# Whole feature tiles instead of half tiles in layer 1's modulation products on TensorE

## The chip, the cores and the metric

One core of a Trainium2 chip runs the whole program as one launch. The time is device microseconds of that core, the median of three runs; lower is better. The engines are named as the profile names them: PE (TensorE's matmuls), PEld (its weight loads), DVE (VectorE), ACT (ScalarE), POOL (GpSimd) and SP (SyncE).

## The reference, cut to what matters

A two layer network with 1024 features works on 512 latent and 256 context tokens. Layer 0 mixes tokens with a gated linear recurrence, layer 1 with latent attention; each is followed by a gated MLP. Everything is modulated: six vectors of 1024 features a layer, each for two conditions (c and c_ctx), come from

```python
silu_c = jax.nn.silu(c)
mod_lat = jnp.split((silu_c @ ada_w[i] + ada_b[i])[:, None, :], 6, axis=-1)
mod_ctx = jnp.split(silu_cc @ ada_w[i] + ada_b[i], 6, axis=-1)
h_lat = _modulate(_rmsnorm(x, norm_mix_g[i]), mod_lat[0], mod_lat[1])
x = x + mod_lat[2] * o_lat
```

`ada_w` is 2 x 1024 x 6144 in float32. Channels 0 and 1 (shift and scale of the first norm) are needed for both conditions in layer 1; its channels 2 to 5 are needed for the latent tokens alone.

## The kernel before, in words

Every matrix product is done in float32 by three passes over a high and a low part (`hh`/`hl`, `wh`/`wl`, `ah`/`al`). Activations are held with the features on the 128 partitions and the 768 tokens along the free axis. Weights come in on SP's queue as `raw` tiles, ACT copies their high part (L108), DVE or POOL subtracts to the low part (L119). The order of the program is written out by hand; each engine works its own instructions off in that order.

The modulation vectors are made in small steps that `ada_step` (L583) puts between other products. `adas` (L225, L227) lists the weight tiles in the order of their use: whole tiles of 128 x 1024 for layer 0's channels 2 to 5, half tiles of 128 x 512 for layer 1, in the order channel, half, k (the eight blocks of 128 input features). `ada_fill` (L232) issues their loads on POOL's queue (L239 for half tiles, L242 for whole ones), up to `used + bufs` tiles ahead; a new load takes the buffer of the tile read longest ago, so it waits for that tile's readers. In layer 0's MLP there are three buffers for half tiles.

`ada_product` (L563) is the step on PE: `csil[:, k, :]` (128 x 32) is the stationary operand, and four matmuls for the four feature quarters of a tile write to four groups of 32 partitions of `psada`, accumulated over k. `ada_sum` (L533) is the step on DVE for one condition alone, one multiply and add over 512 columns (L538 for k = 0, L540 else), whose sum `ada_add` (L544) brings across partitions with the matmuls of L554. Layer 1's channels 0 and 1 go through PE, its channels 2 to 5 through DVE. After a channel's last k `ada_copy` (L558) copies `psada` to SBUF on ACT (L560); `ada_evac` (L508) transposes it on PE (L519) at the third `ada_step` after that and adds the bias on DVE (L525). `ada_until` (L596) does at once what is missing up to a channel.

Layer 0's MLP is `ffn0` (L1136). Four hidden tiles are made plainly (`plain`, L1263), the others two by two blocks by a Strassen scheme of seven products (`pair`, L1224; its matmuls L1166). Six groups of 4, 2, 4, 4, 4, 4 hidden tiles follow each other; behind each group the eight output tiles m = 0 to 7 add their part of the result (L1212, residuals L767). Six PSUM banks hold output tiles, two for each. Layer 1's steps stand in these places: one after each of the plain tiles 1, 2 and 3 (L1288 to L1297), two in each pair while channels 0 and 1 last (`on_pe`, L1222; L1234 and L1246), one otherwise, and behind every output tile (L1333):

```python
on_pe = lambda: ada_state["used"] < 8 * KT
ada_step(1 if nh < 4 or on_pe() else 2)
```

In front of the last group's output tiles stands `ada_until(1, 4)` (L1307).

Of the kernel before, what the change touches and what calls it, by code (L numbers as in the profile page):

```python
# [12 lines left out]
ALU = mybir.AluOpType  # L13
# [4 lines left out]
KT = D // P  # L18
# [127 lines left out]
def kernel(ctx, tc, x, c, ctx_in, c_ctx, ada_w, ada_b, norm_mix_g, norm_ffn_g, ffn_w_in,  # L146
# [4 lines left out]
    act, dve, pe = nc.scalar, nc.vector, nc.tensor  # L151
# [34 lines left out]
    def ps_aux(name):  # L186
        return psx.tile([P, 512], F32, name=name, tag="aux")
# [36 lines left out]

    adas = [(0, ch, k) for ch in range(2, 6) for k in range(KT)]  # L225

    adas += [(1, ch, k, half) for ch in range(6) for half in range(2) for k in range(KT)]  # L227
    N_ADA = [4 * KT, 14 * KT, 16 * KT]
    ada_tiles = {}
    ada_state = {"loaded": 0, "used": 0, "evac": None, "sums": None, "bufs": NB_ADA}  # L230

    def ada_fill(eng=nc.gpsimd):  # L232
        while ada_state["loaded"] < min(N_ADA[0], ada_state["used"] + ada_state["bufs"]):
            i = ada_state["loaded"]
            l, ch, k, *half = adas[i]
            if half:
                c0 = ch * D + half[0] * 512
                t = ada_state["pool"].tile([P, 512], F32, name=f"ada{i}", tag="ada", bufs=3)
                eng.dma_start(t, ada_w[l, k * P:(k + 1) * P, c0:c0 + 512])  # L239
            else:  # L240
                t = ada_pool.tile([P, 1024], F32, name=f"ada{i}", tag="ada")
                eng.dma_start(t, ada_w[l, k * P:(k + 1) * P, ch * D:(ch + 1) * D])  # L242
            ada_tiles[i] = t
            ada_state["loaded"] += 1
# [209 lines left out]
    csil = const.tile([P, KT, 32], F32, name="csil")  # L454
# [15 lines left out]
    mod = const.tile([P, 2, 6, 2, KT], F32, name="mod")  # L470
    gm = const.tile([P, 4, 2, KT], F32, name="gm")
    adab = lambda l, ch: cols_b[:, l * 48 + ch * 8:l * 48 + ch * 8 + 8]
# [5 lines left out]
    ada_ps = {}  # L478
# [29 lines left out]
    def ada_evac(wait=False):  # L508

        if ada_state["evac"] is None:  # L510
            return
        i, l, ch, sb = ada_state["evac"]
        if wait and ada_state["calls"] < 2:
            ada_state["calls"] += 1
            return
        ada_state["evac"] = None
        px = ps_aux(f"adax{i}")
        for cc in range(2):
            pe.transpose(px[:, cc * P:(cc + 1) * P], sb[:, cc * P:(cc + 1) * P], ident)  # L519

        order = "p (c j) -> p c j" if l and ch < 2 else "p (j c) -> p c j"
        n = dict(c=2, j=4)
        pv = px[:, :256].rearrange("p (c j r) -> p c j r", r=32, **n)
        for v in range(2):
            dve.tensor_tensor(mod[:, l, ch, v, :].rearrange(order, **n), pv[:, :, :, v],  # L525
                              adab(l, ch).rearrange(order, **n), op=ALU.add)
        if ch in (1, 4):
            w = l + (2 if ch == 4 else 0)
            for v in range(2):
                dve.scalar_tensor_tensor(gm[:, w, v, :], mod[:, l, ch, v, :], 1.0, gcol(w),  # L530
                                         op0=ALU.add, op1=ALU.mult)

    def ada_sum(i, t, l, ch, k, half):  # L533


        total, col = acc[:, :512], csil[:, k, 0:1]
        if k == 0:
            dve.tensor_scalar(total, t, col, None, op0=ALU.mult)  # L538
        else:
            dve.scalar_tensor_tensor(total, t, col, total, op0=ALU.mult, op1=ALU.add)  # L540
        if k == KT - 1:
            ada_state["sums"], ada_state["calls"] = (i, l, ch, half, total), 0

    def ada_add():  # L544
        if ada_state["sums"] is None:
            return
        i, l, ch, half, total = ada_state["sums"]
        ada_state["sums"] = None
        if half == 0:
            ada_ps["half"] = psa.tile([P, 512], F32, name=f"psada{i}", tag="ada")  # L550
        ps = ada_ps["half"]
        for j in range(2):
            r = 64 * half + 32 * j
            pe.matmul(ps[r:r + 32, :256], pick[:, 0, :], total[:, j * 256:(j + 1) * 256], start=True, stop=True)  # L554
        if half == 1:
            ada_copy(i, l, ch, ps)

    def ada_copy(i, l, ch, ps):  # L558
        sb = ada_state["sb"](i)
        act.activation(sb, ps[:, :256], AF.Copy)  # L560
        ada_state["evac"], ada_state["calls"] = (i, l, ch, sb), 0

    def ada_product(i, t, l, ch, k, half=None):  # L563

        n = 256 if half is None else 128
        if k == 0 and not half:
            ada_ps[0] = psa.tile([P, 512], F32, name=f"psada{i}", tag="ada")
        o = (half or 0) * n
        for j in range(4):
            pe.matmul(ada_ps[0][32 * j:32 * j + 32, o:o + n], csil[:, k, :], t[:, j * n:(j + 1) * n],  # L570
                      start=k == 0, stop=k == KT - 1)
        if k == KT - 1 and half != 0:
            ada_copy(i, l, ch, ada_ps[0])

    def ada_one():
        ada_fill()
        i = ada_state["used"]
        l, ch, *f = adas[i]
        (ada_sum if l and ch > 1 else ada_product)(i, ada_tiles.pop(i), l, ch, *f)
        ada_state["used"] += 1  # L580
        ada_fill()

    def ada_step(n=1):  # L583

        if ada_state["sums"]:
            ada_state["calls"] += 1
            if ada_state["calls"] < 2:
                return
            ada_add()
        else:  # L590
            ada_evac(True)
        for _ in range(n):
            if ada_state["used"] < N_ADA[0] and not ada_state["sums"]:
                ada_one()

    def ada_until(l, ch):  # L596
        n = sum(1 for a in adas if a[:2] <= (l, ch)) - ada_state["used"]
        for _ in range(n):
            ada_add()
            ada_evac()  # L600
            ada_one()
        if n >= 0:
            ada_add()
            ada_evac()
# [361 lines left out]
    gel, used = {}, []  # L966
# [169 lines left out]
    def ffn0(na, nb, nxt):  # L1136
        ga, gb = na.group, nb.group
        with ExitStack() as es:
# [64 lines left out]
            def out_tile(c, m, groups, ks, ps=None):  # L1203
                h0, nh, outs = s0_out[c]
                per = 8 // nh
                wh, wl = st.get(outs[m // per])
                ps = ps or {g[0]: ps_bank(f"fo0{c}{m}{g[0]}")[:, :g[1].stop - g[1].start] for g in groups}
                for k in ks:
                    o = k * (1024 // nh) + m % per * P
                    for q, (w, x) in enumerate(((wh, ah), (wh, al), (wl, ah))):  # L1210
                        for v, s in groups:
                            pe.matmul(ps[v], w[:, o:o + P], x[:, k, s], start=k == 0 and q == 0,  # L1212
                                      stop=k == nh - 1 and q == 2)
                return ps
# [7 lines left out]
            on_pe = lambda: ada_state["used"] < 8 * KT  # L1222
# [79 lines left out]
            for c, (h0, nh, outs) in enumerate(s0_out):  # L1302
                for j in range(max(h0, PLAIN0), h0 + nh):
                    pair(j, j - h0, j == h0 + nh - 1)
                lastp = c == len(s0_out) - 1
                if lastp:
                    ada_until(1, 4)  # L1307
                    for m in range(KT):
                        ps = out_tile(c, m, (ga,), range(nh))
                        residual(m, lambda s: ps[1], 0, 5, ga, True)  # L1310
                        if m == 0:
                            st.flush()
                    st.low_engine = nc.gpsimd

                    def last(m):
                        ps = out_tile(c, m, (gb,), range(nh))
                        residual(m, lambda s: ps[0], 0, 5, gb, True)
                        out_done(c, m)

                    boundary([lambda m=m: last(m) for m in range(KT)], nxt, at=(1, 2, 1))  # L1320
                    return

                n0 = nh - 1 if c else 2
                three = [out_tile(c, m, (gb, ga), range(n0)) for m in range(3)]
                for m in range(KT):
                    if m < 3:
                        ps = out_tile(c, m, (gb, ga), range(n0, nh), three[m])
                    else:
                        ps = out_tile(c, m, (gb, ga), range(nh))
                    for g in (gb, ga):  # L1330
                        residual(m, lambda s: ps[g[0]], 0, 5, g, False)
                    out_done(c, m)
                    ada_step(1 if nh < 4 or on_pe() else 2)  # L1333

    na1 = Norm(1, 1, 0, CTXG, hh, hl, "m1a")
    nb1 = Norm(1, 1, 0, LATG, hh, hl, "m1b")
# [419 lines left out]
```

## Time and profile before

| what | value |
|---|---|
| runs of before, us | 1565.91, 1568.83, 1569.62; median 1568.83 |
| the profiled execution, us | 1571.79 |
| its span from the first to the last instruction, us | 1569.9 |
| PE busy, us | 1512.2 |
| DVE, ACT, POOL busy, us | 934.2, 675.9, 281.5 |
| mean granted clock of TensorE | 0.985 |

The profile is of one execution, a little above the median of the runs. A busy PE isn't PE at its peak, since the ends of matmuls are modelled; a product's price is therefore read from the starts of the instructions around it. A matmul in float32 leaves two records. In a line of the timeline the first number is the start, the second how long the merged instructions last, and the bracket tells how long the engine was idle before and what ended that.

### The profile page before, as it was taken

Reading aid. Unit: us, or ns where it says so; the run is one execution under the profiler, and the core shown is the slowest. Engines: PE = TensorE matmul, PEld = TensorE weight load, DVE = VectorE, ACT = ScalarE, POOL = GpSimd, SP = SyncE. Lnnn points to the kernel's source line nnn. Section 1 sums busy time; section 2 is a strip of 40 time slices with the busy share of each in tenths; the row PEclk is TensorE's granted clock in tenths of the full one; section 3 lists DMA queues with packets and bytes.
Section 4 is the critical chain, followed back from the end, with each engine's and each line's share of the span. In section 5 each row is a group of like instructions: output and inputs, shape, how many; then the busy total and the mean of one; then the engine's idle time right before and its main releaser. Section 6 shows DMA issues by size and latency. Waiting matters only on the chain.

```text
span 1569.9 us, 21629 instructions
## 1 busy us (share of the span) xinstructions
PE 1512.2 (96%) x8903; PEld 1321.4 (84%) x8903; DVE 934.2 (60%) x1397; ACT 675.9 (43%) x989; POOL 281.5 (18%) x261
## 2 busy tenths in 40 slices
PE   7999998979999999999999998999998999999998
PEld 5877876868878898999989887899998888888887
DVE  5766778686855657767587457666537543233234
ACT  5486555734423241433424343766644322232223
POOL 3223333242010101001010332111144100000002
PEclk9999999989999999999999999999999999999999
DMA  9434333131233334333242112110112433223222
GB/s 359 127 108 135 108 122 120 59 103 48 68 108 114 104 112 128 114 114 122 94 141 64 51 56 69 29 43 28 54 54 75 161 118 104 81 98 117 81 69 93
DMA packets 134995, 155.14 MB, mean 99 GB/s; under 512 B 6252, under 2 KB 112353, under 8 KB 134897
## 3 DMA queue, kind: packets, MB, share of 16 engines
q1 hardware_dynamic: 122272, 112.21, 22.3%
q0 software_dynamic: 12320, 41.02, 8.2%
q8 instruction: 70, 1.15, 0.3%
q10 hardware_dynamic: 304, 0.53, 0.1%
q14 instruction: 29, 0.23, 0.0%
HBM read 151.64 MB, written 2.10 MB: 98 GB/s over the span
## 4 chain that ended last, share of the span: by engine, by line
PE 82%; DVE 11%; ACT 4%; issue 1%; DMA 1%; SPq 0%; POOL 0%; DVEq 0%; ACTq 0%; POOLq 0%
PE f L791 14%; PE fo L1212 11%; PE x L1166 10%; PE fo L791 8%; PE z L1166 5%; PE lo L791 3%; PE s L1555 3%; PE ga L791 2%; PE wo L791 2%; PE y L1166 2%; PE o L1597 2%; PE p L791 2%; PE g L791 2%; DVE yc L899 1%; PE t L1573 1%
## 5 line engine op out<-in xcount | busy, mean ns | idle before, releaser
L108 ACT ACTIVATE wh<-raw 128x1024 fp32r<-128x1024 f32 (+3 forms) x247 | 208.5, 871 | 203.9 <-PE fo L1212 64.5
L119 POOL TENSOR_TENSOR wl<-raw,wh 128x1024 fp32r<-128x1024 f32 (+3 forms) x66 | 157.5, 2397 | 328.8 <-ACT wh L108 328.6
L119 DVE TENSOR_TENSOR wl<-raw,wh 128x1024 fp32r<-128x1024 f32 (+2 forms) x181 | 169.3, 948 | 11.8 <-ACT wh L108 11.8
L767 DVE SCALAR_TENSOR_TENSOR xT<-fo,mod,xT 128x512 f32<-128x512 f32 (+1 forms) x124 | 74.1, 626 | 129.8 <-PE fo L1212 66.2
L239 POOL DMA_DIRECT2D ada<-in_ada_w_dram x96 | 51.7, 539 | 465.3 <-PE psada L570 217.9
L791 PE MATMUL f<-hh,wh 128*128 128x512 f32 x320 | 124.7, 390 | 0.0
L791 PE MATMUL f<-hh,wl 128*128 128x512 f32 x320 | 124.5, 389 | 0.0
L791 PE MATMUL f<-hl,wh 128*128 128x512 f32 x320 | 124.5, 389 | 0.0
L785 POOL TENSOR_TENSOR acc<-acc,sq 128x256 f32<-128x256 f32 (+1 forms) x52 | 50.7, 975 | 374.1 <-ACT sq L783 371.9
L1212 PE MATMUL fo<-ah,wh 128*128 128x512 f32 (+1 forms) x352 | 98.3, 345 | 0.9 <-DVE g L1273 0.8
L1212 PE MATMUL fo<-al,wh 128*128 128x512 f32 (+1 forms) x352 | 95.8, 338 | 0.4 <-DVE al L1201 0.4
L1212 PE MATMUL fo<-ah,wl 128*128 128x512 f32 (+1 forms) x352 | 95.3, 337 | 0.0
L1109 DVE TENSOR_TENSOR sg<-sg,f 128x512 f32<-128x512 f32 x20 | 13.7, 687 | 116.4 <-ACT sg L1108 116.4
L1108 ACT ACTIVATE sg<-f 128x512 f32<-128x512 f32 x20 | 12.0, 599 | 148.3 <-PE f L791 148.3
L791 PE MATMUL fo<-ah,wh 128*128 128x512 f32 (+1 forms) x200 | 73.0, 365 | 0.0
L791 PE MATMUL fo<-ah,wl 128*128 128x512 f32 (+1 forms) x200 | 72.7, 364 | 0.0
L791 PE MATMUL fo<-al,wh 128*128 128x512 f32 (+1 forms) x200 | 72.7, 364 | 0.0
L791 PEld LDWEIGHTS f<-hh,wh 128*128 128x128 f32 x320 | 60.1, 188 | 13.2 <-issue 0.8
L791 PEld LDWEIGHTS f<-hh,wl 128*128 128x128 f32 x320 | 60.1, 188 | 12.6
L791 PEld LDWEIGHTS f<-hl,wh 128*128 128x128 f32 x320 | 60.1, 188 | 12.4
L1212 PEld LDWEIGHTS fo<-ah,wh 128*128 128x128 f32 x352 | 56.2, 188 | 12.8 <-issue 4.6
L1212 PEld LDWEIGHTS fo<-al,wh 128*128 128x128 f32 x352 | 56.2, 188 | 8.0 <-DVE al L1201 0.7
(490 smaller groups left out, 4023.3 us busy)
## 6 DMA issues: line engine op xcount, KB each, us to landing
raw<-in_ffn_w_in_dram SPq DMA_DIRECT2D x26, 1024.0 KB, 4.9
ada<-in_ada_w_dram POOLq DMA_DIRECT2D x96, 256.0 KB, 3.1
raw<-in_ffn_w_out_dram SPq DMA_DIRECT2D x19, 1024.0 KB, 4.9
raw<-in_ffn_w_in_dram SPq DMA_DIRECT2D x36, 512.0 KB, 4.7
ada<-in_ada_w_dram POOLq DMA_DIRECT2D x30, 512.0 KB, 4.4
ada<-in_ada_w_dram SPq DMA_DIRECT2D x32, 256.0 KB, 5.5
raw<-in_lru_w_in_dram SPq DMA_DIRECT2D x10, 512.0 KB, 5.3
raw<-in_lru_gate_w_dram SPq DMA_DIRECT2D x16, 256.0 KB, 3.2
```

The costliest lines, as they stand in the source:

```text
L108: nc.scalar.activation(dst(hi), src(self.raw[load]), AF.Copy)
L119: self.low_engine.tensor_tensor(dst(lo), src(self.raw[load]), dst(hi).bitcast(F32), op=ALU.subtract)
L239: eng.dma_start(t, ada_w[l, k * P:(k + 1) * P, c0:c0 + 512])
L767: dve.scalar_tensor_tensor(xT[:, m, s], ps(s) if callable(ps) else ps[:, s], mod[:, l, ch, v, m:m + 1], xT[:, m, s], op0=ALU.mult, op1=ALU ...
L785: accs.append(lambda: nc.gpsimd.tensor_tensor(acc[:, s], acc[:, s], sq, op=ALU.add))
L791: pe.matmul(ps[:, off + s.start:off + s.stop], a, b[:, s], start=first and i == 0, stop=last and i == 2)
L899: dve.scalar_tensor_tensor(y[:, s0:s1], ps[:, s0 + o:s1 + o], convw(tap, k), y[:, s0:s1], op0=ALU.mult, op1=ALU.add)
L1166: pe.matmul(ps, w[:, o:o + P], x[:, k0 + k, s], start=first and k == 0 and q == 0, stop=last and k == 3 and q == 2, skip_group_check=not f ...
L1212: pe.matmul(ps[v], w[:, o:o + P], x[:, k, s], start=k == 0 and q == 0, stop=k == nh - 1 and q == 2)
L1555: pe.matmul(ps[:, o:o + 384], x, y[:, k0:k1], start=j == 0, stop=j == 4)
L1573: pe.transpose(ps[:, j * P:(j + 1) * P], prs[h, b][:, j // 3, j % 3 * P:(j % 3 + 1) * P], ident)
L1597: pe.matmul(ps[:, :256], x[:, t % 4, hs], y[:, t, :], start=t == 0 and j == 0, stop=t == NT - 1 and j == 2)
```

## The change

For layer 1's channels 0 and 1 the order of `adas` becomes channel, k, half. `ada_product` takes a list of tiles: one whole tile for layer 0, two half tiles for layer 1, and does four matmuls of 256 columns with either. A step of layer 1's products so uses two half tiles, which are still loaded one by one. The special order of features in `ada_evac` goes. Behind output tiles, while channels 0 and 1 last, the call stands at every second m (groups of four hidden tiles) or every third (others).

```diff
-    adas += [(1, ch, k, half) for ch in range(6) for half in range(2) for k in range(KT)]
+    adas += [(1, ch, k, half) for ch in range(2) for k in range(KT) for half in range(2)]
+    adas += [(1, ch, k, half) for ch in range(2, 6) for half in range(2) for k in range(KT)]
...
-    def ada_product(i, t, l, ch, k, half=None):
-
-        n = 256 if half is None else 128
-        if k == 0 and not half:
+    def ada_product(i, ts, l, ch, k):
+
+        if k == 0:
             ada_ps[0] = psa.tile([P, 512], F32, name=f"psada{i}", tag="ada")
-        o = (half or 0) * n
+        n = 4 // len(ts)
         for j in range(4):
-            pe.matmul(ada_ps[0][32 * j:32 * j + 32, o:o + n], csil[:, k, :], t[:, j * n:(j + 1) * n],
+            pe.matmul(ada_ps[0][32 * j:32 * j + 32, :256], csil[:, k, :], ts[j // n][:, j % n * 256:j % n * 256 + 256],
                       start=k == 0, stop=k == KT - 1)
-        if k == KT - 1 and half != 0:
+        if k == KT - 1:
             ada_copy(i, l, ch, ada_ps[0])
 
     def ada_one():
         ada_fill()
         i = ada_state["used"]
-        l, ch, *f = adas[i]
-        (ada_sum if l and ch > 1 else ada_product)(i, ada_tiles.pop(i), l, ch, *f)
-        ada_state["used"] += 1
+        l, ch, k, *half = adas[i]
+        n = 1
+        if l and ch > 1:
+            ada_sum(i, ada_tiles.pop(i), l, ch, k, *half)
+        else:
+            n = 1 + l
+            ada_product(i, [ada_tiles.pop(i + j) for j in range(n)], l, ch, k)
+        ada_state["used"] += n
         ada_fill()
...
     def ada_until(l, ch):
         n = sum(1 for a in adas if a[:2] <= (l, ch)) - ada_state["used"]
-        for _ in range(n):
+        end = ada_state["used"] + n
+        while ada_state["used"] < end:
...
-                    ada_step(1 if nh < 4 or on_pe() else 2)
+                    ada_step(1 if nh < 4 else 2) if not on_pe() or m % (2 if nh == 4 else 3) == 0 else None
```

In `ada_evac` every channel now uses the order `"p (j c) -> p j c"` for `mod` and the bias.

## Rows read from the trace of the kernel before

**Rows 1.** The page: span, and busy time of the engines.
```profile
span 1569.9 us, 21629 instructions
...
PE 1512.2 (96%) x8903; PEld 1321.4 (84%) x8903; DVE 934.2 (60%) x1397; ACT 675.9 (43%) x989; POOL 281.5 (18%) x261
```

**Rows 2.** Stretches: length, PE, PEld, DVE, ACT, POOL busy (count), granted clock, DMA share, GB/s.
```profile
433.20:475.00 41.80, 41.04 (x279) 32.82 (x278) 23.26 (x35) 8.68 (x12) 4.84 (x9) 1.00 0.36 104
...
509.60:528.90 19.30, 19.30 (x151) 14.49 (x150) 12.68 (x25) 2.80 (x5) 4.30 (x8) 1.00 0.35 101
```

**Rows 3.** One tile's instructions (`psada`), and PE's timeline around one half tile.
```profile
L570 PE MATMUL psada<-ada,csil x512: 272/338/403, 60.4 to 600.4; 128*32 128x256 f32 x86, 128*32 128x128 f32 x85
...
442.28 0.51 PE L1212 MATMUL fo<-al,wh 128*128 128x512 f32 x2
442.63 0.51 PE L1212 MATMUL fo<-ah,wl 128*128 128x512 f32 x2
443.07 0.43 PE L570 MATMUL psada<-ada,csil 128*32 128x128 f32 x8
443.43 0.61 PE L1212 MATMUL fo<-ah,wh 128*128 128x512 f32 x2
```

**Rows 4.** PE's timeline around one whole tile of layer 0, and around two.
```profile
59.92 0.51 PE L791 MATMUL p<-hh,wl 128*128 128x512 f32 x2
60.36 0.64 PE L570 MATMUL psada<-ada,csil 128*32 128x256 f32 x8
60.93 0.50 PE L791 MATMUL g<-hh,wh 128*128 128x512 f32 x1
...
87.50 0.51 PE L791 MATMUL g<-hh,wl 128*128 128x512 f32 x2
87.94 1.07 PE L570 MATMUL psada<-ada,csil 128*32 128x256 f32 x16
88.94 0.50 PE L791 MATMUL ga<-uh,wh 128*128 128x512 f32 x1
```

**Rows 5.** PE's timeline at the start of group 0's output tiles.
```profile
434.40 0.50 PE L1212 MATMUL fo<-ah,wh 128*128 128x512 f32 x1 [0.76 <-DVE g L1273]
```

**Rows 6.** POOL's and SP's timelines; landing: loads from 440 to 480, that at 449.1.
```profile
443.83 0.54 POOL L239 DMA_DIRECT2D ada<-in_ada_w_dram  x1 [9.32 <-PE psada L570]
...
DMA to landing us min/median/max: 2.9/2.9/5.6
...
DMA to landing us min/median/max: 5.6/5.6/5.6
...
448.04 0.99 SPq L350 DMA_DIRECT2D raw<-in_ffn_w_in_dram  x2
```

**Rows 7.** PE's timeline: one sum brought across partitions (two feature quarters).
```profile
619.84 0.62 PE L554 MATMUL psada<-acc,pick 128*32 128x256 f32 x4
```

**Rows 8.** Stretches (columns as in Rows 2): two idle times of PE, and what followed.
```profile
127.20:130.10 2.90, 0.04 (x1) 0.04 (x1) 1.86 (x5) 0.91 (x2) 0.00 (x0) 1.00 0.09 31
130.10:134.20 4.10, 3.73 (x11) 2.93 (x12) 2.64 (x3) 2.67 (x3) 0.00 (x0) 0.59 0.00 0
...
870.70:872.90 2.20, 0.04 (x2) 0.00 (x0) 1.29 (x3) 2.06 (x3) 0.00 (x0) 1.00 0.21 62
872.90:880.00 7.10, 7.08 (x59) 7.08 (x60) 4.21 (x10) 1.53 (x4) 1.47 (x2) 1.00 0.27 74
```

**Rows 9.** PE's and DVE's timelines in front of the last group's output tiles.
```profile
869.84 0.34 PE L1166 MATMUL x<-hh,wl 128*128 128x384 f32 x1
...
872.92 0.44 PE L519 MATMUL adax<-ident,acc 128*128 128x128 f32 x2 [2.18 <-ACT acc L560]
873.12 0.36 PE L1212 MATMUL fo<-ah,wh 128*128 128x256 f32 x1
...
871.68 0.96 DVE L1201 TENSOR_TENSOR al<-g,ah 128x768 fp32r<-128x768 f32 x1 [0.91 <-ACT ah L1200]
```

**Rows 10.** One line's instructions: the sums on DVE.
```profile
L540 DVE SCALAR_TENSOR_TENSOR acc<-ada,csil,acc x56: 741/750/754, 607.2 to 1263.3; 128x512 f32<-128x512 f32 x56
```

More of the change, by code (lines that the diff above doesn't have):

```diff
@@ L519, in ada_evac @@
             pe.transpose(px[:, cc * P:(cc + 1) * P], sb[:, cc * P:(cc + 1) * P], ident)
-        order = "p (c j) -> p c j" if l and ch < 2 else "p (j c) -> p c j"
-        n = dict(c=2, j=4)
-        pv = px[:, :256].rearrange("p (c j r) -> p c j r", r=32, **n)
+        pv = px[:, :256].rearrange("p (c j r) -> p j c r", c=2, j=4)
         for v in range(2):
-            dve.tensor_tensor(mod[:, l, ch, v, :].rearrange(order, **n), pv[:, :, :, v],
-                              adab(l, ch).rearrange(order, **n), op=ALU.add)
+            dve.tensor_tensor(mod[:, l, ch, v, :].rearrange("p (j c) -> p j c", j=4), pv[:, :, :, v],
+                              adab(l, ch).rearrange("p (j c) -> p j c", j=4), op=ALU.add)
         if ch in (1, 4):
```

## The prediction

> **What bounds the kernel now.** I read the page's busy times first. PE is busy for 1512.2 of 1569.9 us [rows 1], so whatever is put into PE's queue, work or wait, moves the end unless PE would have waited there anyway. Then I read the stretches in which layer 1's products run. From the first output tiles of group 0 (433.2 us) to the first Strassen pair, PE is busy for 41.04 of 41.80 us at the full clock; while group 1's output tiles are made (509.6 to 528.9) it is never idle, and DVE is busy for 12.68 of 19.30 us [rows 2]. So in this stage DVE, ACT and POOL have time left and PE has none. The reader is to see in these two groups that a stop of PE here has no later idle time to be made up in.
>
> **The change part by part.** The profiled execution took 1571.79 us (its span is 1569.9), 2.96 us above the median of 1568.83. I sum changes on 1571.8 and take the same sum off the median.
>
> *The products.* The 512 matmul records are two for each matmul: 256 for layer 0's 32 whole tiles and 256 for layer 1's 32 half tiles [rows 3]. A half tile costs what it adds between two output matmul pairs: 443.43 - 442.63, less the 0.35 that separates such pairs (442.63 - 442.28), is 0.45 us [rows 3]. Layer 0 shows the price of what replaces it. A whole tile adds 60.93 - 59.92 - 0.35 = 0.66 us and two in a row 88.94 - 87.50 - 0.35 = 1.09 us [rows 4]: 0.43 for each tile, and some 0.23 for entering and leaving. One of the 32 half tiles costs nothing now, since behind it PE waits 0.76 us for DVE at 434.40 [rows 5]; the whole tile that comes there is 0.21 longer and stays inside that wait. So 31 x 0.45 = 13.95 us go.
>
> What comes is read from the edited call. Three steps after the plain pairs (one of them hidden), two in each of pairs 4 and 5, and m = 0 of group 1 take one tile: 7 x 0.66 = 4.62. In group 0 four heads are processed, so the call there is `ada_step(2)` at m = 0, 2, 4 and 6: the edit dropped `or on_pe()`, which kept this at one. Four doubled steps are 4 x 1.09 = 4.36. Together 3 + 8 + 4 + 1 = 16 tiles. Without any wait PE gains 13.95 - 8.98 = **4.97 us**.
>
> *The wait in the doubled step.* The pool still has three half tile buffers, and `ada_fill` loads up to `used + 3`. A doubled step eats four half tiles. The first product takes two of the three that are there; only then are the buffers refilled; the second product takes the third and one that has just been asked for. POOL can't ask before PE has read the buffer: each such load waits for `psada` [rows 6]. For a half tile the load is issued 0.76 us after the first matmul (443.83 - 443.07, [rows 3, 6]); a whole tile's burst is 0.64 long instead of 0.43 [rows 3, 4], so 0.97. From issue to landing the nine loads of this stretch took 2.9 (lowest), 2.9 (median) and 5.6 us (highest) [rows 6]; the long one was issued at 449.1, a microsecond behind two weight loads on SP at 448.04 [rows 6]. Those weight loads hang on the output tile m = 1, and the doubled step of m = 2 still follows it, so I give m = 2 the long landing and the other three the short one. Behind the landing PE still has two of four feature quarters to do. Two last as long as four side by side: the record of a two-quarter sum is 0.62 long [rows 7], that of a whole tile 0.64, and PE goes on 60.93 - 60.36 = 0.57 us after its start [rows 4]. The wait is then landing + 0.97 + 0.57, less the 1.00 that two tiles take unstopped (88.94 - 87.94): 2.9 gives 3.4, 5.6 gives 6.1. Four of them are 3 x 3.4 + 6.1 = **16.3 us**. Queued behind the waiting matmul is everything on PE, and the residuals on DVE wait for PE; nothing that runs meanwhile shortens PE's own work. Ends of this term: all four short (13.6), all four long (24.4).
>
> The Trainium skill (DMA: Bandwidth & Descriptors, Anatomy of one DMA) fits a GpSimd load as 2.0 us plus its bytes at 436 GB/s, which for 256 KB is an estimate of 2.6 us; by that the four waits would be 4 x 3.1 = 12.4 us. No load of rows 6 was that quick, so the rows decide.
>
> *The clock.* A stop of this length has a price behind it. PE was idle from 127.2 to 130.1 (busy 0.04 of 2.90) and the 4.1 us after that ran at a granted 0.59 of full speed, in part at 1.2 GHz: 0.41 x 4.1 = 1.7 us lost. A shorter idle time, 870.7 to 872.9, was followed by 1.00 [rows 8]. The idle part of our wait is about landing + 0.97 - 1.07 (the doubled burst lasts 1.07), so 2.8 to 5.5 us: nearer to 2.9 than to 2.2. I take 1.7 for each, **6.8 us**, and keep 0 as the other end. [...]
>
> *The sums come earlier.* Tile 64, the first for DVE, is reached at group 1's m = 1 and not in group 2's output tiles. Counting steps on, layer 1's channel 4 is then finished and copied in group 4's output tiles, and `ada_until(1, 4)` in front of the last group finds nothing. There PE now waits 2.18 us for ACT [rows 9]. Without that wait the first output tile starts at 870.0 rather than 873.12, but the last of its four hidden tiles needs `al`, which DVE ends at 871.68 + 0.96 = 872.64 [rows 9]. Twelve matmuls of 0.12 ended at 874.55; now they end near 872.9. Of the 1.65 gained, 0.57 and 0.23 for the sum's matmuls, and some 0.1 for the two transposes, are paid elsewhere, where PE is full: **0.8 us** net.
>
> *At nothing.* DVE does seven sums more in group 1's output tiles, at most 7 x 0.75 = 5.25 us [rows 10], beside 12.68, in 19.3 - 8 x 0.45 + 0.66 = 16.4 us: 1.5 too many. Their cover is the six PSUM banks (three output tiles ahead) and the lighter pairs after them; if that is gone it costs up to 1.5. The loads on POOL's queue are as many and as large as before and POOL does nothing else here. SP's weight loads follow PE as before. The reordering in `ada_evac` changes addresses only.
>
> Sum: 16.3 + 6.8 - 4.97 - 0.8 = +17.3. 1571.8 becomes 1589.1, and the median 1586.1.
>
> **The rivals.** *The half tile is back in time (faster).* If the second product's last half tile has landed when PE gets there, nothing waits: -5.8, 1563.0. It decides at the doubled steps, and breaks even where the four stops with their clock come to 5.8 us, 1.4 each, so landings of about 0.9 us. For it speaks that POOL and half of the DMA capacity are free (share 0.36, [rows 2]); against it the 2.9 us [rows 6].
>
> *The clock stays up.* Stops as above, no loss behind them: 1586.1 - 6.8 = 1579.3. For it: our shortest idle time lies between the 2.2 us that cost nothing and the 2.9 that did [rows 8].
>
> *Every stop is a long one.* Two loads are asked for at once now, and weight loads move with PE: four waits of 6.1 and the clock give 24.4 + 6.8 - 5.8 = +25.4, 1594.2, and with DVE's 1.5 1595.7. For it speaks the one row in nine at 5.6.
>
> *The step isn't doubled*, because the call takes one tile a place after all: then products spill into group 2, no wait arises, and PE's gain of 31 x 0.45 - 15 x 0.66 = 4.1 gives 1564.7. The condition in the diff speaks against it.
>
> **How the numbers follow.** The forecast gets 0.63, the clock that stays up 0.17, long stops 0.12, the landing in time 0.05, the step that isn't doubled 0.03. A measurement of this kernel can tell about 0.3% (4.7 us) from no change. The first three cases lie over that (lowest +7.8: four short stops, no clock loss, all gains), the last two at -4.1 and -5.8, one of them inside the bound. Some hundredths stand for half of my waits being wrong: slower 0.91, same 0.04, faster 0.05. The range goes from 1576, four short stops without clock loss, to 1596, the long stops with DVE's price.
>
> **What would show it.** The profile after should have 128 records of L570 fewer; 16 products; four waits of PE for a DMA into `ada`, in group 0's output tiles, of 3 to 6 us each, every one in its second tile; a lower granted clock behind them; the first sum on DVE right behind group 1's m = 0; and no wait for ACT in front of the last group's output tiles. I am wrong if PE shows no wait for `ada` there, or if these are under 1.5 us each. If they are as I say and the clock stays at 1.00, the second rival holds.

## The result, and the profile after

The changed kernel takes 1587.01 us (median of 4 runs, 1583.17 to 1590.87), the kernel before 1569.22 (4 runs); the ratio is 1.0117, with a 95% interval of 1.0088 to 1.0147. It is slower by 17.8 us, where +17.3 was forecast. Its profiled execution took 1587.94 us, with a span of 1586.1.

The page of the changed kernel, busy times. The program's lines in `ffn0` stand three further on than before (L1212 is now L1215), and L570 is now L567, L554 is L552, L560 is L558, L540 is L538, L239 is L240 and L350 is L351.

```profile
PE 1516.7 (96%) x8775; PEld 1326.7 (84%) x8775; DVE 931.2 (59%) x1397; ACT 676.4 (43%) x989; POOL 281.9 (18%) x261
```

There are 128 PE records fewer than in [rows 1], as forecast. Busy time alone would say that nothing is wrong: 96% as before. What the change did shows in the stretches of its own stage. These are group 0's output tiles, group 1's and group 2's, each from its first output matmul to the first matmul of the next pair; columns are length, then PE, PEld, DVE, ACT and POOL busy (count), granted clock, DMA share and GB/s.

```profile
432.95:495.68 62.73, 48.92 (x256) 37.00 (x257) 19.63 (x29) 6.86 (x11) 9.36 (x18) 0.84 0.35 109
528.22:547.04 18.82, 18.33 (x108) 15.03 (x108) 16.77 (x33) 4.16 (x8) 3.76 (x7) 1.00 0.43 127
606.06:642.25 36.19, 34.48 (x200) 29.65 (x199) 25.28 (x40) 6.11 (x10) 6.06 (x12) 1.00 0.43 129
```

Before, the first of these stretches was

```profile
434.40:472.71 38.31, 38.31 (x257) 30.62 (x257) 20.00 (x30) 6.93 (x11) 3.87 (x8) 1.00 0.38 111
```

So group 0's output tiles take 24.4 us more: PE is idle for 13.8 of 62.73 us, and the granted clock fell from 1.00 to 0.84. All other stages of layer 0's MLP together give 6.9 us back (its whole stretch, from group 0's first output tile to the next layer, went from 474.41 to 491.92 us). The waits of PE between 430 and 640 us in the changed kernel (waited for: us in total, times, longest) name the cause.

```profile
PE psada L567 <- DMA ada<-in_ada_w_dram: 13.3, 4, 5.3
PE psada L552 <- DVE acc L538: 1.7, 1, 1.7
PE fo L1215 <- DVE g L1276: 0.5, 1, 0.5
PE psada L567 <- ACT acc L558: 0.5, 1, 0.5
PE fo L1215 <- DVE al L1204: 0.4, 1, 0.4
```

PE's timeline at the first two doubled steps, m = 0 and m = 2, answers to [rows 3, 4]:

```profile
441.63 1.06 PE L567 MATMUL psada<-ada,csil 128*32 128x256 f32 x12
445.59 0.62 PE L567 MATMUL psada<-ada,csil 128*32 128x256 f32 x4 [2.90 <-DMA ada<-in_ada_w_dram]
446.14 0.94 PE L1215 MATMUL fo<-ah,wh 128*128 128x512 f32 x2
...
452.11 1.06 PE L567 MATMUL psada<-ada,csil 128*32 128x256 f32 x12
458.50 1.07 PE L567 MATMUL psada<-ada,csil 128*32 128x256 f32 x4 [5.34 <-DMA ada<-in_ada_w_dram]
459.50 0.80 PE L1215 MATMUL fo<-ah,wh 128*128 128x512 f32 x1
```

Twelve of sixteen records run at once, the last four wait: one of the four half tiles is not there. The wait for ACT in the table above is at m = 4: there the first product ends channel 0 and the second begins channel 1, and PE waits 0.53 us until ACT has copied `psada`. The half tile came later than that copy, so the copy cost nothing here. POOL's and SP's timelines, with the landing of the loads issued at 442.56 and 453.04, say why; they answer to [rows 6].

```profile
442.56 1.06 POOL L240 DMA_DIRECT2D ada<-in_ada_w_dram  x2 [8.79 <-PE psada L567]
...
DMA to landing us min/median/max: 3.0/3.0/3.0
...
452.31 0.99 SPq L351 DMA_DIRECT2D raw<-in_ffn_w_in_dram  x2
...
453.04 1.59 POOL L240 DMA_DIRECT2D ada<-in_ada_w_dram  x3 [5.99 <-PE psada L567]
...
DMA to landing us min/median/max: 5.4/5.4/5.4
```

The load is issued 0.93 us after the first matmul of the place and lands 3.0 or 5.4 us later; the long one has two weight loads on SP just ahead of it. Behind each stop the clock is down (stretches that begin where the four stops end, columns as above):

```profile
445.60:452.00 6.40, 6.40 (x28) 5.09 (x28) 2.02 (x3) 0.63 (x1) 0.54 (x1) 0.73 0.30 84
458.50:463.30 4.80, 4.80 (x16) 3.40 (x17) 0.00 (x0) 0.00 (x0) 0.54 (x1) 0.50 0.27 87
473.70:477.00 3.30, 3.30 (x11) 2.21 (x12) 0.00 (x0) 0.00 (x0) 0.54 (x1) 0.51 0.40 113
488.20:494.00 5.80, 5.79 (x19) 4.30 (x20) 0.00 (x0) 0.00 (x0) 0.54 (x1) 0.50 0.29 89
```

### The profile page after: what moved, and what is told of

It reads as the page before. It is cut to its first block, busy times and chain, and to the rows that moved or that the text cites. A ratio compares the mean times of both kernels' runs of the same rounds, so it can differ in the third digit from the quotient of the medians.

```text
span 1586.1 us, 21365 instructions
## 1 busy us (share of the span) xinstructions
PE 1516.7 (96%) x8775; PEld 1326.7 (84%) x8775; DVE 931.2 (59%) x1397; ACT 676.4 (43%) x989; POOL 281.9 (18%) x261
## 4 chain that ended last, share of the span: by engine, by line
PE 68%; issue 13%; DVE 12%; ACT 4%; DMA 2%; POOL 1%; SPq 0%; DVEq 0%; POOLq 0%; ACTq 0%
PE f L794 14%; PE fo L794 8%; PE x L1169 7%; PE fo L1215 6%; PE z L1169 4%; PE lo L794 3%; PE s L1558 3%; PE ga L794 2%; PE wo L794 2%; PE o L1600 2%; PE y L1169 2%; PE p L794 2%; PE g L794 2%; DVE yc L902 1%; DMA ada<-in_ada_w_dram 1%
## 5 line engine op out<-in xcount | busy, mean ns | idle before, releaser
L108 ACT ACTIVATE wh<-raw 128x1024 fp32r<-128x1024 f32 (+3 forms) x247 | 208.5, 871 | 208.4 <-PE fo L1215 96.8
L240 POOL DMA_DIRECT2D ada<-in_ada_w_dram x96 | 51.6, 539 | 455.3 <-DVE acc L538 206.4
L1215 PE MATMUL fo<-ah,wh 128*128 128x512 f32 (+1 forms) x352 | 99.6, 349 | 1.1 <-DVE g L1276 0.5
L1215 PE MATMUL fo<-al,wh 128*128 128x512 f32 (+1 forms) x352 | 97.8, 345 | 1.0 <-DVE al L1204 1.0
L1215 PE MATMUL fo<-ah,wl 128*128 128x512 f32 (+1 forms) x352 | 97.3, 343 | 0.0
L1112 DVE TENSOR_TENSOR sg<-sg,f 128x512 f32<-128x512 f32 x20 | 13.8, 688 | 116.7 <-ACT sg L1111 116.7
L1215 PEld LDWEIGHTS fo<-ah,wh 128*128 128x128 f32 x352 | 58.4, 195 | 13.7 <-issue 4.5
L1215 PEld LDWEIGHTS fo<-al,wh 128*128 128x128 f32 x352 | 58.0, 195 | 9.0 <-DVE al L1204 1.5
```

The costliest lines, as they stand in the source:

```text
L108: nc.scalar.activation(dst(hi), src(self.raw[load]), AF.Copy)
L1112: dve.tensor_tensor(sg[:, :n], sg[:, :n], pu[:, off:off + n], op=ALU.mult)
```

## The experiments

The theory is the forecast's: a doubled step eats four half tiles, three are in store, and the fourth is asked for only when PE has read the first, so PE stops for the load and runs at half clock behind it. The rivals are that whole tiles or doubled steps are slow by themselves, that the clock is no part of the price, and that DVE's earlier sums are the bound.

**One tile a place.** Group 0's step isn't doubled; the rest of the program's text is the changed kernel's. The four products left over move to later places, so DVE's first sum starts at 548.23 us instead of 536.45 (606.67 before the change).

```diff
-ada_step(1 if nh < 4 else 2) if not on_pe() or m % (2 if nh == 4 else 3) == 0 else None
+ada_step(1 if nh < 4 or on_pe() else 2) if not on_pe() or m % (2 if nh == 4 else 3) == 0 else None
```

> The doubled steps in group 0 become single ones (every second m still); two products move to pair 6. Theory (a doubled step needs a half tile that was only just asked for): PE waits nowhere for a load into ada, the clock stays at 1.00 through group 0, and the time is that of before less 31 x 0.45 - 15 x 0.66 = 4.1 us and 0.8 us at the last group, some 1564.5 us. Rival (whole tiles as such, their order of loads or the earlier sums on DVE make it slow): still above 1575 us, without long waits.

Measured: 1563.55 us (7 runs), ratio to the kernel before 0.9964 (0.9950 to 0.9979). All waits of PE from 430 to 640 us:

```profile
PE fo L1215 <- DVE g L1276: 0.5, 1, 0.5
PE fo L1215 <- DVE al L1204: 0.4, 1, 0.4
PE psada L552 <- DVE acc L538: 0.3, 1, 0.3
```

No wait for `ada`, and group 0's output tiles take 37.00 us at a clock of 1.00:

```profile
434.56:471.56 37.00, 37.00 (x224) 30.10 (x225) 19.63 (x29) 6.48 (x10) 5.06 (x10) 1.00 0.41 129
```

The rival falls: whole tiles, their order and sums that are earlier than before, if less early than in the changed kernel, are a gain of 0.36%; with the doubled step it is a loss. The next run keeps the early sums.

**Four half tiles in store.** The doubled steps stay.

```diff
+                if ch < 2 and i % 4 == 3:
+                    t = acc[:, :512]
+                else:
+                    t = ada_state["pool"].tile([P, 512], F32, name=f"ada{i}", tag="ada", bufs=3)
...
+        if ada_state["bufs"] > 2:
+            ada_state["bufs"] = 4 if ada_state["used"] < 8 * KT else 3
```

> Doubled steps stay, but there are four half tiles in store while the products last (the fourth lies in the first 512 columns of acc, which are free then). Theory: all four half tiles of a doubled step have landed before it, the four waits of 2 to 5 us and the low clock behind them go, 1564 to 1566 us (DVE may still hold PE up by 1.7 us in group 2). Rival (doubling a step stops PE by something else: the copy of psada on ACT, the residuals on DVE): waits remain in group 0 and the time stays above 1575 us.

Measured: 1565.00 us (8 runs), ratio 0.9972 (0.9962 to 0.9982). Waits of PE from 430 to 640 us (the lines stand five further on than in the changed kernel):

```profile
PE psada L557 <- DVE acc L543: 2.1, 1, 2.1
PE fo L1220 <- DVE g L1281: 0.5, 1, 0.5
PE psada L572 <- ACT acc L563: 0.5, 1, 0.5
PE psada L572 <- DMA ada<-in_ada_w_dram: 0.4, 1, 0.4
PE fo L1220 <- DVE al L1209: 0.4, 1, 0.4
```

With one more half tile in store, 13.3 us of waiting for `ada` become 0.4, and group 0's output tiles take 40.50 us (432.55 to 473.05) instead of 62.73. The stops of 3 to 6 us are not the doubled step's own; they come of too little in store. Some 2 us stay in group 0: read from the starts, the place at m = 2 takes 1.26 us longer than the unstopped 1.00, as a load is still late there, and the one at m = 4 takes 0.74 us longer, where the copy of `psada` on ACT no longer hides behind a load. The longest wait left has nothing to do with group 0: DVE's, in group 2.

**Half tiles, doubled.** The kernel before with the changed kernel's places in group 0.

```diff
-ada_step(1 if nh < 4 or on_pe() else 2)
+ada_step(1 if nh < 4 else 2) if not on_pe() or nh < 4 or m % 2 == 0 else None
```

> The kernel before, with half tiles and their order untouched, but with the places of group 0 as in the changed kernel: every second m, two steps each. Two half tiles are eaten at a place, and three are in store. Theory: no wait for a load, four pairs of half tiles save some 0.2 us each in entering and leaving, so the time of before or 1 us less. Rival (a doubled step in a place stops PE whatever it eats): waits of some us at m = 0, 2, 4, 6 and over 1575 us.

Measured: 1568.68 us (10 runs), ratio 0.9996 (0.9984 to 1.0008): no difference. Here no wait of PE from 430 to 640 us is for `ada`, as a place eats two of three. The same doubling costs nothing with half tiles, where group 0's output tiles take 37.10 us (431.32 to 468.42) against 38.31 before. With whole tiles and three in store it costs 22 us against four in store (62.73 and 40.50).

**Filler in the stops.** Ten matmuls whose result nobody reads, between the two products of a doubled step.

```diff
+    def filler():
+        px = ps_aux("filler")
+        for _ in range(10):
+            pe.matmul(px, hh[:, 0, 0:P], hh[:, 1, 0:512], start=True, stop=True)
...
+                if q and adas[ada_state["used"]][:2] in ((1, 0), (1, 1)):
+                    filler()
                 ada_one()
```

> The changed kernel with ten matmuls of 128x512 whose result nobody reads (some 2.35 us) between the two products of a doubled step. Theory with the clock: they lie inside the waits, which get shorter by as much (0.5 to 1 us left, 3 at m = 2), and PE's clock doesn't fall behind them; of the 8.6 us that the half clock cost, most goes: 1578 to 1581 us. Rival (the clock is no price of the stops): as long as the changed kernel, 1587 us, or longer by the added matmuls.

Measured: 1579.97 us (4 runs), ratio to before 1.0064 (1.0049 to 1.0079). PE still waits 3.9 us for `ada`, 2.4 of them at m = 2:

```profile
PE psada L567 <- DMA ada<-in_ada_w_dram: 3.9, 4, 2.4
```

and group 0's output tiles, at a granted 0.97, take

```profile
433.80:491.07 57.27, 53.33 (x297) 39.65 (x297) 19.60 (x29) 6.83 (x11) 9.32 (x18) 0.97 0.38 120
```

PE does 40 matmuls more and the stretch, whose first output matmul starts at 433.76, is 5.4 us shorter than the changed kernel's 62.73. The loads come no sooner for it: from the first matmul of a place to its last four records PE takes 18.8 us in the four places together, against 18.2 in the changed kernel. So what went is the half clock: it is a price of its own, and the rival falls. One stretch of low clock is left, behind the longest stop.

**A step behind every m.** One whole tile at each output tile of group 0.

```diff
-ada_step(1 if nh < 4 else 2) if not on_pe() or m % (2 if nh == 4 else 3) == 0 else None
+ada_step(1 if nh < 4 or on_pe() else 2)
```

> One whole tile behind every output tile of group 0, as before the call stood. Theory: a place needs one half tile that was asked for at the place before; it is there 0.97 + 2.9 = 3.9 us after that place began, and the place after m = 0 comes 0.66 + 2.22 = 2.9 us later. So one wait of about 1 us at m = 1, up to 2.5 at m = 2 if weight loads come in between, none at m = 3 to 7 (4.4 us apart), no lower clock, some 1565 to 1568 us. Rival (a load is late whenever two half tiles are used at a place): waits at every m.

Measured: 1564.91 us (one run). PE at m = 0 and m = 1:

```profile
442.38 0.64 PE L567 MATMUL psada<-ada,csil 128*32 128x256 f32 x8
442.95 0.61 PE L1215 MATMUL fo<-ah,wh 128*128 128x512 f32 x2
...
446.64 0.63 PE L567 MATMUL psada<-ada,csil 128*32 128x256 f32 x4 [0.79 <-DMA ada<-in_ada_w_dram]
```

The second place waits 0.79 us, where 1 was worked out. At m = 2, where weight loads could have made a wait, none is listed. One of 0.3 us came at m = 3, where none was expected (1.1 us in two waits in all); read from the starts, that place took 1.21 us instead of 0.57, and its load, issued at 450.45, needed 4.8 us to land. In this one run, as in the changed kernel, PE waits by what is missing between the spacing of two places and the way of a load; which load will be a long one was not foreseen.

**Doubled steps at odd m.** m = 1, 3, 5, 7 in place of 0, 2, 4, 6.

```diff
-ada_step(1 if nh < 4 else 2) if not on_pe() or m % (2 if nh == 4 else 3) == 0 else None
+ada_step(1 if nh < 4 else 2) if not on_pe() or (m % 2 == 1 if nh == 4 else m % 3 == 0) else None
```

> The changed kernel with group 0's doubled steps at m = 1, 3, 5, 7 instead of 0, 2, 4, 6. Theory (the 5.3 us wait at m = 2 is long because two weight loads, set off by the output tile m = 1, are issued 0.3 to 0.7 us before its load): the load at m = 1 is now issued before those weight loads, so all four waits are 2 to 3.5 us and at most one stretch of low clock is over 3.4 us. Rival (which landing is long is chance, or the second place is always the long one): one wait of 5 us or more remains.

Measured: 1580.43 us (one run). Waits of PE from 430 to 640 us, and SP's weight loads:

```profile
PE psada L567 <- DMA ada<-in_ada_w_dram: 9.5, 3, 3.2
PE psada L567 <- ACT acc L558: 2.8, 1, 2.8
...
445.65 0.99 SPq L351 DMA_DIRECT2D raw<-in_ffn_w_in_dram  x2
```

No single wait is over 3.2 us, and the longest place, from its first matmul to the next output matmul, takes 5.28 us, where the changed kernel's at m = 2 takes 7.39. The load that the first one waits for was issued at 444.26, ahead of the weight loads, and landed in 3.3 us; the one issued at 445.56 beside them took 5.8, but nobody waited for it. In all eight traces without filler a load issued within 1.1 us of these two weight loads took 4.8 to 5.8 us to land, and the first one in group 0, well ahead of them, 2.8 to 3.7. So the long stop at m = 2 was the weight loads' doing. One stop here is put down to ACT: the channel's copy of `psada` stood behind a weight part (L108) that itself waited 2.1 us for DVE, and the half tile landed 0.8 us after it, so it would have stopped PE anyway.

This run holds a surprise for the clock. Its stretches behind the first, second and fourth stop (3.20, 3.09 and 3.17 us idle):

```profile
447.60:452.00 4.40, 4.40 (x25) 3.48 (x26) 1.79 (x4) 0.00 (x0) 0.54 (x1) 1.00 1.01 316
...
458.80:463.00 4.20, 4.16 (x15) 3.27 (x16) 0.00 (x0) 0.00 (x0) 0.54 (x1) 0.59 0.37 113
...
488.50:493.00 4.50, 4.50 (x30) 3.43 (x31) 0.75 (x2) 0.49 (x1) 1.28 (x3) 1.00 0.75 275
```

Two of these three cost no clock at all, while 2.90 us in the changed kernel did. The third stop, 2.81 us for ACT and 0.8 for the load behind it, was followed by the half clock too: the output matmul pairs behind it start 0.80 and 0.65 us apart, where 0.45 and 0.35 are the full clock's.

**The sum later.** Four half tiles in store, and the add across partitions one place later.

```diff
-            if ada_state["calls"] < 2:
+            if ada_state["calls"] < 3:
                 return
             ada_add()
```

> Four half tiles in store as in the run with four buffers, and the matmuls that bring a DVE sum across partitions wait for one place more (three calls instead of two). Theory (with the sums earlier, PE reaches the add in group 2 while DVE still works off two sums, residuals and weight parts): the wait of PE for DVE in group 2, 2.1 us with four buffers, goes, the rest stays, some 1563 us. Rival (DVE has too much work in group 2 as a whole): the wait moves to an output tile that waits for its PSUM bank, and the time stays at 1565 us.

Measured: 1561.02 us (5 runs), ratio to before 0.9944 (0.9930 to 0.9957). Waits of PE from 430 to 640 us:

```profile
PE psada L572 <- DMA ada<-in_ada_w_dram: 0.6, 1, 0.6
PE fo L1220 <- DVE g L1281: 0.5, 1, 0.5
PE psada L572 <- ACT acc L563: 0.5, 1, 0.5
PE fo L1220 <- DVE al L1209: 0.4, 1, 0.4
```

DVE's wait is gone and no other took its place; group 2's output tiles take 34.11 us (585.08 to 619.19) instead of 36.61 with four half tiles alone. DVE had time enough; the add only came too soon. This version beats the kernel before and the changed one.

## Why the prediction was right, point by point

**The stops: right, 16.5 us for 16.3.** From the first matmul of a doubled step to the next output matmul PE took 446.14 - 441.63 = 4.51 us at m = 0, 7.39 at m = 2, 4.92 at m = 4 and 4.97 at m = 6, where 1.00 is unstopped: 17.8 us, of which 1.3 are the last two quarters at half clock in three places (1.00 instead of 0.57). Issue after 0.93 us (0.97 forecast), three landings of 3.0 or less and one of 5.4 (2.9 and 5.6 forecast), the long one at m = 2. Four buffers take all but some 2 us of the stops away, odd places shorten the long one.

**The clock: right, some 7.6 us for 6.8, for a reason that is only half right.** Group 0's stretch grew by 24.4 us; the places themselves add 4 x 1.19 - 8 x 0.55 = 0.4 (next point) and the stops 16.5, which leaves 7.6. It is a remainder, but the starts bear it out: behind the stops output matmul pairs start 0.64 us apart in place of 0.35 until the clock is back. That each stop is followed by the half clock, as the forecast took it, is not so: with odd places two of four weren't. What decides which, these runs don't tell.

**The products: the right sign, too small.** The forecast's 4.97 us took a place's price up to the next output matmul and stopped there. But the matmul after it is late too. PE's timeline of the kernel before, continued from [rows 3], and a whole tile in the changed kernel:

```profile
443.43 0.61 PE L1212 MATMUL fo<-ah,wh 128*128 128x512 f32 x2
443.88 0.40 PE L1212 MATMUL fo<-al,wh 128*128 128x512 f32 x1
```

```profile
396.18 0.52 PE L794 MATMUL f01u<-hh,wl 128*128 128x512 f32 x2
396.63 0.64 PE L567 MATMUL psada<-ada,csil 128*32 128x256 f32 x8
397.19 0.61 PE L794 MATMUL f02g<-hh,wh 128*128 128x512 f32 x2
397.65 0.51 PE L794 MATMUL f02g<-hl,wh 128*128 128x512 f32 x2
```

443.88 - 443.43 is 0.45, not 0.35. A half tile's place so costs 443.88 - 442.63 - 2 x 0.35 = 0.55 us and a whole tile's 397.65 - 396.18 - 2 x 0.35 = 0.77; two tiles then 1.19. Of 31 x 0.55 = 17.1 us, 7 x 0.77 + 4 x 1.19 = 10.2 come back: 6.9 us gained, not 4.97. The run with one tile a place confirms these prices: 38.31 - 8 x 0.55 + 4 x 0.77 = 36.99 us for group 0's output tiles, and 37.00 were measured. The 0.1 us is paid at each place, so going from 31 places to 11 saves more than the forecast had.

**At nothing: wrong place.** In group 1, where the forecast saw DVE 1.5 us short, PE waited for none of its sums: DVE is busy for 16.77 of 18.82 us there. In group 2 it did:

```profile
626.40 0.74 DVE L538 SCALAR_TENSOR_TENSOR acc<-ada,csil,acc 128x512 f32<-128x512 f32 x1
...
627.93 0.75 DVE L538 SCALAR_TENSOR_TENSOR acc<-ada,csil,acc 128x512 f32<-128x512 f32 x1 [0.79 <-DMA ada<-in_ada_w_dram]
...
628.74 0.63 PE L552 MATMUL psada<-acc,pick 128*32 128x256 f32 x4 [1.71 <-DVE acc L538]
```

The earlier start puts the end of the first sum on the short output tiles of group 2, where PE comes to the add while DVE is still at the last tile of the sum, which waited 0.79 us for its own load. PE waits 1.71 us, which the forecast had at 0 with 1.5 as the end of its range. Both misses nearly cancel.

**The last group: right.** The wait for ACT in front of its output tiles is gone; PE now waits there for `ah` and `al`, 0.46 and 0.61 us. From the end of group 4's output tiles to the next layer the time falls from 97.05 to 95.54 us, 1.5 for the forecast's gross 1.65.

Two of the 31 places lie ahead of group 0's output tiles. In the stretch from these tiles to the next layer the products so give 29 x 0.55 - 5 x 0.77 - 4 x 1.19 = 7.3 us back. The terms as measured, 16.5 + 7.6 + 1.7 - 7.3, with the forecast's 0.8 for the last group, whose net price no run measures by itself, come to 17.7 us, and the stretch grew by 17.5. The two profiled executions as a whole are only 16.2 us apart, since the changed kernel came to group 0's first output matmul 1.45 us earlier. Over all nine traces that moment lies between 431.32 and 434.56 us, so this can't be put down to the change.

That the total came out within 0.5 us of the forecast is in part luck: the products gave 1.9 us more than forecast, DVE's wait took 1.7 and the clock 0.8 more.

## What to carry to other kernels

Before a step is made to eat more at a time, count what it eats against what lies in store: a buffer that is refilled only after the step has read it costs the whole way of a load, here some 4 us, at each place, and often TensorE's clock behind it. Spacing and store are two cures for the same want, and either one turned 1.2% of loss into 0.3 to 0.4% of gain. And price an insertion up to the second instruction behind it, not the first.

## What the runs showed that was not expected

Idle times of 3.20 and 3.17 us were followed by a granted clock of 1.00, one of 2.90 us by the half clock: the length of a stop alone doesn't tell its price on the clock. And ten matmuls put into each stop, useless ones, made the kernel 7.0 us faster (1587.01 to 1579.97): group 0's output tiles ran at a granted 0.97 with them, 0.84 without.
